# Output products end with the lower, then the upper columns; the third weight tile's low part goes behind the residual; three mixer units begin with a product in two halves

## The chip, the cores and the metric

The kernel runs on one core of a Trainium2 chip. The core has a matrix engine (TensorE, PE in the profile, with its weight loads as PEld), a vector engine (VectorE, DVE), a scalar engine (ScalarE, ACT), a general engine (GpSimd, POOL) and a queue engine for transfers (SyncE, SP). The metric is the device time of one execution, in microseconds (us); lower is better.

## What is computed

A decoder trunk of two layers on 256 positions of 1024 columns, in float32. Each layer is a half-step feed-forward block, a mixing block with two branches (a Mamba-2 style scan and a gated delta rule) on the same normalised input, and a second half-step feed-forward block.

```python
for l in range(DEPTH):                                   # DEPTH = 2
    h = h + 0.5 * swiglu(rms_norm(h, ffn1_norm[l]), ffn1_w_in[l], ffn1_w_out[l])
    u = rms_norm(h, mix_norm[l])
    (z_s, xbc, dt_s, qkv, z_d, b_d, a_d, gate_s, gate_d) = split(u @ w_in[l])
    y_s = mamba2_branch(z_s, xbc, dt_s, ...)
    y_d = deltanet_branch(qkv, z_d, b_d, a_d, ...)
    merged = sigmoid(gate_s) * (y_s @ ssm_w_branch[l]) + sigmoid(gate_d) * (y_d @ dn_w_branch[l])
    h = h + merged @ w_out[l]
    h = h + 0.5 * swiglu(rms_norm(h, ffn2_norm[l]), ffn2_w_in[l], ffn2_w_out[l])
return rms_norm(h, final_norm)
```

## The kernel before

**Weights.** All weights are streamed from memory once, as tiles of 128 x 1024 float32 (512 KB each). A tile is loaded into one of five raw buffers (`wraw`), and split into a high part `whi` (ScalarE, line 67) and a low part `wlo`, the raw tile less the high part (VectorE, line 70); there are five buffers of each. `prep` issues both; `take` hands a tile to the products and prepares the tiles ahead. Activations are split in the same way (`uW`, `gh`/`gl`, `mh`/`ml`). Every product of two matrices is three products on TensorE: high by high, high by low, low by high (`mm3` with 512 columns at a time, lines 318 to 320; `mm3w` with 256 columns, lines 323, 328 and 329).

**Two shapes of stage.** `tok_chunk` takes tiles in groups and multiplies both halves of the 256 positions (t = 0, then t = 1) by them, twelve products of 512 columns a tile. `chan_chunk` computes 256 channels for all positions from two tiles: 2 x 8 x 3 = 48 products of 256 columns, into one accumulator. The mixer's k, q, v, d, b and x units are each one `chan_chunk` (tiles `kk`, `qq`, `vv`, `zd`, `bc`, `xs` in the profile), its z and gate units `tok_chunk` (tile `t`). In the feed-forward blocks the `chan_chunk` products write `fc`.

**A product in two halves.** `mm3w(cut=True)` issues the second product of the three (high by low) as two products of 128 columns each (lines 325 and 326) instead of one of 256. `chan_chunk` does so once, at its fifth product (`a == 0 and kt == 1`), if it is asked to. Only the feed-forward blocks ask: for the third `fc` unit, and for the first one behind each group of block products.

**Output products and the joint.** A block ends with output products `o`: `out_chunks` takes the last five tiles (NSPL = 5) as one group, t = 0 first and then t = 1, into four accumulators `po[t][n]` (n = 0 the lower, n = 1 the upper 512 columns). For t = 0 all five tiles run for n = 0 and then for n = 1. For t = 1 each tile runs for n = 0 and then n = 1, unless `split` is set (only the last block of all). `state["sums"]` keeps each sum's last product; the transposes of t = 0 are held behind the sixth sum of t = 1, so that twelve products follow them.

Behind the output products comes what this document calls a joint (`norm_in` with `add`, five in the program: after the first feed-forward block of each layer, after each mixer, and between the layers). For each t: the residual add `h` for both n (VectorE, line 73), two squares (`junk`, ScalarE), a small add `zz` (VectorE), a power (`zz`, GpSimd), two scalings `hn` (VectorE), eight transposes `hnT` on TensorE (line 284), and the split of the transposed input into `uW` (high part ScalarE, low part VectorE). All of this has high priority in the scheduler that fixes the order of each engine's instructions when the program is built. The first tiles of the next stage are split around it: with n the index of the next stage's first tile, tiles n and n + 1 stand behind `hn` of t = 0, the third tile n + 2 behind `uW` of t = 0, the fifth tile n + 4 behind the squares and `hn` of t = 1; the fourth has no such edge. `tc.issue_after(ins)` adds an edge to the program's order: what is issued inside stands behind `ins` on the engine of `ins`.

**The mixer.** `ORDER` gives its units. Those around the change are, in the order of the program: `k1 k0 q1 k2 k3 K1 K0 q3 q0`, later `z30 v1 z31 Q2 v2 V0 I v3 V1 I V3 I Q1 V2 d0 R R R b3 R b2`, and later `S1 x20 T1 o x21`. A capital or single letter is a step without weights (transposes, small products, the inversion `I`, the recurrence `R`, the scan `S`/`T`). In the inversion 16 x 16 blocks go through memory, and come back as `T` and `TT`; the products `yb` read them.

Of the kernel before, what the change touches and what calls it, by code (L numbers as in the profile page):

```python
# [11 lines left out]
ALU = mybir.AluOpType  # L12
# [18 lines left out]
NSPL = 5  # L31
# [21 lines left out]
def trunk_kernel(ctx, tc, x, wst, wsm, norms, lpar, rpar, cst, out):  # L53
# [12 lines left out]
    def act(o, i, func=AF.Copy, **kw):  # L66
        return A.activation(out=o, in_=i, func=func, **kw)  # L67

    def tt(o, a, b, op):
        return V.tensor_tensor(out=o, in0=a, in1=b, op=op)  # L70

    def stt(o, a, s, b, op0, op1):
        return V.scalar_tensor_tensor(out=o, in0=a, scalar=s, in1=b, op0=op0, op1=op1)
# [6 lines left out]
    def f(ap):  # L80
        return ap.bitcast(F32)
# [67 lines left out]
    for _, _, need in plan:  # L149
        m, room = need, NRAW  # L150
# [4 lines left out]
            m += 1  # L155
        limit.append(m)
    n_forms = len(plan)
    state = {"loaded": 0, "prepped": 0, "taken": 0, "last": None, "hold": False, "behind": {}, "first": 0}
    raws, halves = {}, {}

    def tile_of(i):
# [2 lines left out]
    def add_to(r, i):  # L164
        G.dma_start(out=r[:], in_=tile_of(i), accum_op=ALU.add)  # L165
# [14 lines left out]
    def prep(i):  # L180
        kind, js, _ = plan[i]
        hi = wpool.tile([P, 1024], F32R, tag="whi", name="whi", bufs=NSPL)
        lo = wpool.tile([P, 1024], F32R, tag="wlo", name="wlo", bufs=NSPL)
        r = raws[js[0]]
        with ExitStack() as behind:
            for ins in state["behind"].pop(i, ()):
                behind.enter_context(tc.issue_after(ins))
            act(hi[:], r[:])
            if kind in ("q0", "q1"):
                to, by = (raws[k][:] for k in js[1:])  # L190
                tt(to, to, by, ALU.add)
            tt(lo[:], r[:], f(hi[:]), ALU.subtract)
        if kind == "q3":
            add_to(r, js[1])
        for k in {"q0": (js[0], js[-1]), "q1": (), "q3": ()}.get(kind, (js[0],)):
            raws.pop(k)
        halves[i] = (hi, lo)

    def ahead(key, n, fn):
        while state[key] < n:  # L200
            fn(state[key])
            state[key] += 1
# [88 lines left out]
    def norm_in(nw, add=None):  # L291

        place_input()
        for t in range(2):
            with tc.high_priority(offset=PRI), ExitStack() as behind:
                if add:
                    add(t)
                    if t == 0:
                        behind.enter_context(tc.issue_after(state["sums"][5].ins))
                ins, done = rms_chain(t, nw)  # L300
            if t == 0:
                state["hold"] = False
                n = state["taken"]
                if not add:
                    ahead("prepped", n + 1, prep)
                    with tc.issue_after(done[0].ins), tc.issue_after(done[1].ins):
                        ahead("prepped", n + START, prep)
                with tc.issue_after(ins.ins):
                    ahead("prepped", n + 2, prep)
                if add:  # L310
                    state["behind"][n + 2] = [d.ins for d in done]
            elif add:

                state["behind"][n + 4] = (state["square"].ins, ins.ins)
                state["input"] = done

    def mm3(ps, lh, ll, rh, rl, start, stop):
# [30 lines left out]
    def chan_chunk(ps, cut=False):  # L348

        ws = [take(), take()]  # L350
        for a in range(2):
            for q in range(2):
                wh, wl = ws[q]
                for k in range(4):
                    kt = 4 * q + k
                    c0 = k * 256 + a * P
                    mm3w(
                        ps[:, a * 256 : (a + 1) * 256],
                        wh[:, c0 : c0 + P],
                        wl[:, c0 : c0 + P],  # L360
                        uTh[:, kt, :],
                        uTl[:, kt, :],
                        kt == 0,
                        kt == KT - 1,
                        cut and a == 0 and kt == 1,
                    )

    def out_chunks(ps, stat, ks, last, group=1, split=False, first=None):

        for g0 in range(0, len(ks), group):  # L370
            kk = ks[g0 : g0 + group]
            ws = [(k, take()) for k in kk]
            for t in range(2):
                order = [(k, n) for n in range(2) for k in range(len(kk))]
                if t == 1 and not split:
                    order = [(k, n) for k in range(len(kk)) for n in range(2)]
                state["sums"] = []
                for k, n in order:
                    k, (wh, wl) = ws[k]
                    sh, sl = stat(k, t)  # L380
                    ins = mm3(
                        ps[t][n][:], sh, sl,
                        wh[:, n * 512 : (n + 1) * 512], wl[:, n * 512 : (n + 1) * 512],
                        k == 0 if first is None else first and t == n == 1, k == last,
                    )
                    state["sums"].append(ins)

    def residual(po, nw):
        def add(t):
            for n in range(2):  # L390
                hv = h[:, t, n * 512 : (n + 1) * 512]
                stt(hv, po[t][n][:], 0.5, hv, ALU.mult, ALU.add)

        if nw is None:
            return add
        norm_in(nw, add)
# [155 lines left out]
    def mixer(l, nxt):  # L552
# [201 lines left out]

        def k_unit(hp):
            ps = accb("kk")
            chan_chunk(ps)
            for a in range(2):
                conv(ps[:, a * S : (a + 1) * S], 2 * hp + a, kP[:, hp, :, a, :], False)

            def rest():
                ktb, nb = turned(kP, hp)
                ts(kq[:, hp], nb[:], EPS, ALU.add)
                c1 = small([P, 4], "c1")
                V.reciprocal(out=c1[:], in_=kq[:, hp])
                tt(c1[:], c1[:], Bp[:, hp], ALU.mult)
                stt(c3n[:, hp], c1[:], -1.0, eG[:, hp], ALU.mult, ALU.mult)
                kkb = trb("kkb")
                own(kkb, kP, kP, hp)
                kk = s2.tile([P, 4, 64], F32, tag="s2", name="kk")  # L770
                for c in range(4):
                    act(kk[:, c], kkb[:, c * 64 : (c + 1) * 64], scale=c1[:, c : c + 1])
                for a in range(2):
                    rows_ = slice(64 * a, 64 * a + 64)
                    qev["ins"] = tt(Q[rows_, 4 * hp : 4 * hp + 4, rows_], dN[rows_, 4 * hp : 4 * hp + 4], kk[rows_], ALU.mult)
                for c in range(3):
                    act(kd[:, c, hp, :], ktb[:, c * P : (c + 1) * P], scale=dT[:, 4 * hp + c, 63:64])
                rsqrt(c2[:, hp], kq[:, hp], [P, 4])
                G.tensor_tensor(out=c2[:, hp], in0=c2[:, hp], in1=Bp[:, hp], op=ALU.mult)
                yield  # L780

            return rest()
# [19 lines left out]

        def v_unit(hp):
            ps = accb("vv")
            chan_chunk(ps)
            vP = s2.tile([P, 4, 2, 64], F32, tag="s2", name="vP")
            for a in range(2):
                conv(ps[:, a * S : (a + 1) * S], 16 + 2 * hp + a, vP[:, :, a, :], False)

            def rest():  # L810
                vtb = trb("vtb")
                for c in range(4):
                    PE.transpose(vtb[:, c * P : (c + 1) * P], vP[:, c].rearrange("p a i -> p (a i)"), ident)
                for c in range(4):
                    act(vb[:, c, hp, :], vtb[:, c * P : (c + 1) * P], scale=c2[:, hp, c : c + 1])
                yield

            return rest()
# [167 lines left out]
        late = {}  # L986
# [49 lines left out]
        def xs_unit(g, i):  # L1036
            if i == 0:
                xsT[g] = slots.tile([P, 4, S], F32, tag=("sG", "sI")[g % 2], name="xsT")
            ps = accb("xs")
            chan_chunk(ps)  # L1040
            for a in range(2):
                conv(
                    ps[:, a * S : (a + 1) * S], 32 + 4 * g + 2 * i + a,
                    xsT[g][:, 2 * i + a].rearrange("p (c i) -> p c i", c=4), True,
                )
# [166 lines left out]
        m = tg[1]  # L1212
        ps = branch("s", 8, ss_T)
# [20 lines left out]
        po = [[accb("o"), accb("o")] for _ in range(2)]  # L1234
# [7 lines left out]
    for l in range(DEPTH):  # L1242
        ffn(norm_vec(3 * l + 1))
        mixer(l, norm_vec(3 * l + 2))
        add = ffn(norm_vec(3 * l + 3) if l + 1 < DEPTH else None)
# [145 lines left out]
```

## Time and profile before

| | |
|---|---|
| median of 3 runs | 1561.14 us (1560.59 to 1561.25) |
| profiled execution | 1561.29 us, its span 1559.5 us |
| TensorE busy | 1533.0 us, 98% of the span |
| VectorE busy | 1209.6 us, 78% |
| ScalarE busy | 945.0 us, 61% |
| TensorE clock granted, mean | 0.997 |

The profile shows one execution. Times in it count from the span's start. Each engine works through its own queue in a fixed order, and waits where an input of the next instruction isn't ready. Products on TensorE are pipelined: the time between two starts is the pace, and the duration of one is longer than that. `x64` is a count of instructions, and `<-` behind an idle time names what ended it.

### The profile page before, as it was taken

To read this page: it belongs to the slowest core of one execution; us is meant where nothing else is said; L and a number is where in the kernel's file an instruction comes from. 1 tells how busy PE (TensorE), PEld (TensorE's weight loads), DVE (VectorE), ACT (ScalarE), POOL (GpSimd) and SP (SyncE) were. 2 spreads that over 40 slices of the span, in tenths; PEclk is the share of its full clock that TensorE was granted. 3 is DMA by queue.
4 is the path that set the end of the run, shared out by engine and by line. 5 is a ranking of instruction groups with operands and counts; after the bars stand their busy time and mean duration, and the time that the engine had idled before them with its cause. 6 is when DMAs were issued, how large, how long until landed. Compare 5 with 4: busy or idle time off the path is not lost.

```text
span 1559.5 us, 29036 instructions
## 1 busy us (share of the span) xinstructions
PE 1533.0 (98%) x11452; PEld 1387.0 (89%) x11452; DVE 1209.6 (78%) x1840; ACT 945.0 (61%) x1534; POOL 95.9 (6%) x108
## 2 busy tenths in 40 slices
PE   8999999999999999999999999999999999999998
PEld 7999879999888888999789998899998888889996
DVE  5778868967899766778677787699579996667786
ACT  5555667766665645556555566686756665455564
POOL 0000110000000000000100011000000000000010
PEclk9999999999999999999999999999999999999999
DMA  8877765553565585577966687655435547856784
GB/s 287 257 251 237 246 213 181 171 163 116 180 207 173 179 255 193 185 251 228 323 209 205 219 257 238 200 188 176 132 123 199 193 161 221 247 173 197 231 251 155
DMA packets 103438, 322.50 MB, mean 207 GB/s; under 512 B 23349, under 2 KB 24325, under 8 KB 102278
## 3 DMA queue, kind: packets, MB, share of 16 engines
q1 hardware_dynamic: 96390, 299.68, 57.0%
q0 software_dynamic: 6912, 20.97, 7.8%
q8 instruction: 90, 1.47, 0.4%
q14 instruction: 46, 0.38, 0.1%
HBM read 314.50 MB, written 1.92 MB: 203 GB/s over the span
## 4 chain that ended last, share of the span: by engine, by line
PE 83%; DVE 7%; DMA 3%; issue 3%; ACT 3%; POOL 1%; SPq 0%; POOLq 0%; ACTq 0%; DVEq 0%
PE fc L329 9%; PE fc L323 9%; PE fc L328 9%; DVE wlo L70 3%; PE t L319 3%; PE t L318 3%; PE t L320 3%; PE b L320 3%; PE b L319 3%; PE b L318 2%; PE o L320 2%; PE o L319 2%; PE o L318 2%; DMA wraw<-in_wst_dram 2%; PE p L319 2%
## 5 line engine op out<-in xcount | busy, mean ns | idle before, releaser
L70 DVE TENSOR_TENSOR wlo<-wraw,whi 128x1024 fp32r<-128x1024 f32 x504 | 611.1, 1221 | 174.5 <-ACT whi L67 166.9
L67 ACT ACTIVATE whi<-wraw 128x1024 fp32r<-128x1024 f32 x504 | 527.1, 1058 | 273.9 <-PE fc L328 87.7
L329 PE MATMUL fc<-uW,wlo 128*128 128x256 f32 x1280 | 354.8, 277 | 0.0
L323 PE MATMUL fc<-uW,whi 128*128 128x256 f32 x1280 | 354.1, 277 | 0.0
L328 PE MATMUL fc<-uW,whi 128*128 128x256 f32 x1260 | 348.2, 276 | 0.0
L323 PEld LDWEIGHTS fc<-uW,whi 128*128 128x128 f32 x1280 | 240.3, 188 | 0.8
L329 PEld LDWEIGHTS fc<-uW,wlo 128*128 128x128 f32 x1280 | 240.5, 188 | 0.0
L328 PEld LDWEIGHTS fc<-uW,whi 128*128 128x128 f32 x1260 | 236.5, 188 | 0.8
L318 PE MATMUL t<-whi,uW 128*128 128x512 f32 x256 | 102.0, 400 | 0.0
L319 PE MATMUL t<-wlo,uW 128*128 128x512 f32 x256 | 100.7, 393 | 0.6 <-DVE wlo L70 0.4
L320 PE MATMUL t<-whi,uW 128*128 128x512 f32 x256 | 100.8, 394 | 0.0
L318 PE MATMUL b<-whi,bh 128*128 128x512 f32 x192 | 76.3, 399 | 0.3 <-ACT bh L67 0.3
L319 PE MATMUL b<-wlo,bh 128*128 128x512 f32 x192 | 74.9, 390 | 0.0
L320 PE MATMUL b<-whi,bl 128*128 128x512 f32 x192 | 74.3, 394 | 0.6 <-DVE bl L70 0.6
L323 PE MATMUL xs<-uW,whi 128*128 128x256 f32 x256 | 72.6, 284 | 0.0
L329 PE MATMUL xs<-uW,wlo 128*128 128x256 f32 x256 | 71.1, 278 | 0.0
L328 PE MATMUL xs<-uW,whi 128*128 128x256 f32 x256 | 70.9, 277 | 0.0
L70 DVE TENSOR_TENSOR wlo<-wsum,whi 128x1024 fp32r<-128x1024 f32 x48 | 58.6, 1221 | 14.7 <-ACT whi L67 13.8
L67 ACT ACTIVATE whi<-wsum 128x1024 fp32r<-128x1024 f32 x48 | 50.8, 1058 | 28.4 <-PE fc L328 23.8
L318 PE MATMUL o<-whi,gh 128*128 128x512 f32 x160 | 63.8, 399 | 1.9 <-ACT whi L67 1.9
L319 PE MATMUL o<-wlo,gh 128*128 128x512 f32 x160 | 63.9, 399 | 1.6 <-DVE wlo L70 1.6
L165 POOL DMA_DIRECT2D wsum<-in_wst_dram x32 | 28.1, 878 | 584.3 <-DVE wlo L70 455.1
(320 smaller groups left out, 3429.8 us busy)
## 6 DMA issues: line engine op xcount, KB each, us to landing
wraw<-in_wst_dram SPq DMA_DIRECT2D x520, 512.0 KB, 5.0
wsum<-in_wst_dram POOLq DMA_DIRECT2D x32, 512.0 KB, 7.3
wsum<-in_wst_dram SPq DMA_DIRECT2D x16, 512.0 KB, 7.1
dc<-rdram SPq DMA_DIRECT2D x8, 1024.0 KB, 9.1
nw<-in_norms_dram SPq DMA_DIRECT2D x6, 512.0 KB, 6.3
h<-u POOLq DMA_DIRECT2D x12, 256.0 KB, 6.8
gb<-rdram SPq DMA_DIRECT2D x8, 256.0 KB, 5.7
h<-in_x_dram SPq DMA_DIRECT2D x4, 256.0 KB, 3.0
```

Of the source, the lines that this page charges most:

```text
L67: return A.activation(out=o, in_=i, func=func, **kw)
L70: return V.tensor_tensor(out=o, in0=a, in1=b, op=op)
L165: G.dma_start(out=r[:], in_=tile_of(i), accum_op=ALU.add)
L318: PE.matmul(ps, lh, rh, start=start, stop=False)
L319: PE.matmul(ps, lh, rl, start=False, stop=False)
L320: return PE.matmul(ps, ll, rh, start=False, stop=stop)
L323: PE.matmul(ps, wh, mh, start=start, stop=False)
L328: PE.matmul(ps, wh, ml, start=False, stop=False)
L329: PE.matmul(ps, wl, mh, start=False, stop=stop)
```

## The change

Three things are changed.

1. For t = 1 of a group of five output tiles, the first three tiles still run n = 0, n = 1 each; the last two run both for n = 0 (the lower columns), then both for n = 1 (the upper columns). The sum of the lower columns is complete six products before the end instead of three.
2. `residual`'s `add` returns its last instruction, and `norm_in` keeps that of t = 1 under the index of the third tile of the next stage. When this tile is prepared, the instructions behind that point, the low part on VectorE above all, stand behind the residual add in VectorE's order.
3. `chan_chunk` is asked for the product in two halves in units k1, v2 and x20 of the mixer, in both layers: six more products in the program.

```diff
@@ prep
+            if i in state["late"]:
+                behind.enter_context(tc.issue_after(state["late"].pop(i).ins))
             tt(lo[:], r[:], f(hi[:]), ALU.subtract)
@@ norm_in
                 if add:
-                    add(t)
+                    added = add(t)
...
                 state["behind"][n + 4] = (state["square"].ins, ins.ins)
+                state["late"][n + 2] = added
@@ out_chunks
                 order = [(k, n) for n in range(2) for k in range(len(kk))]
                 if t == 1 and not split:
-                    order = [(k, n) for k in range(len(kk)) for n in range(2)]
+                    m = len(kk) - 2 if len(kk) == NSPL else len(kk)
+                    order = [(k, n) for k in range(m) for n in range(2)]
+                    order += [(k, n) for n in range(2) for k in range(m, len(kk))]
@@ residual: add
-                stt(hv, po[t][n][:], 0.5, hv, ALU.mult, ALU.add)
+                ins = stt(hv, po[t][n][:], 0.5, hv, ALU.mult, ALU.add)
+            return ins
@@ k_unit
-            chan_chunk(ps)
+            chan_chunk(ps, hp == 1)
@@ v_unit
-            chan_chunk(ps)
+            chan_chunk(ps, hp == 2)
@@ xs_unit
-            chan_chunk(ps)
+            chan_chunk(ps, (g, i) == (2, 0))
```

More of the change, by code (lines that the diff above doesn't have):

```diff
@@ L157, in trunk_kernel @@
     n_forms = len(plan)
-    state = {"loaded": 0, "prepped": 0, "taken": 0, "last": None, "hold": False, "behind": {}, "first": 0}
+    state = {"loaded": 0, "prepped": 0, "taken": 0, "last": None, "hold": False, "behind": {}, "late": {}, "first": 0}
     raws, halves = {}, {}
```

## The prediction

> **What bounds the kernel now.** I read the page first (engine shares, then the chain that ended last), then TensorE's own waits, then the timeline at the five joints (places where output products end and the next stage begins), then TensorE's products unit by unit in the two mixers.
>
> ```profile
> span 1559.5 us, 29036 instructions
> PE 1533.0 (98%) x11452; PEld 1387.0 (89%) x11452; DVE 1209.6 (78%) x1840; ACT 945.0 (61%) x1534; POOL 95.9 (6%) x108
> PE 83%; DVE 7%; DMA 3%; issue 3%; ACT 3%; POOL 1%; SPq 0%; POOLq 0%; ACTq 0%; DVEq 0%
> ```
>
> TensorE is busy for 98% of the span and carries 83% of the chain. So time comes off in only two ways: TensorE waits less, or its products follow each other faster. The change tries both. The list of TensorE's waits, from 10 us on (so without the start), has one row for the joints:
>
> ```profile
> PE hnT L284 <- DVE hn L73: 4.3, 5, 0.9
> ```
>
> Five waits, one for each joint with a residual before a norm, 4.3 us in all. The timeline of the first joint (start, duration, engine, line, output<-inputs) shows how it arises:
>
> ```profile
> 181.05 13.02 SPq L177 DMA_DIRECT2D wraw<-in_wst_dram  x4
> ...
> 190.75 2.01 ACT L67 ACTIVATE whi<-wraw 128x1024 fp32r<-128x1024 f32 x2
> 191.31 1.28 DVE L70 TENSOR_TENSOR uW<-hnT,uW 128x512 fp32r<-128x512 f32 x2
> 192.51 1.21 DVE L70 TENSOR_TENSOR wlo<-wraw,whi 128x1024 fp32r<-128x1024 f32 x1
> 192.53 0.39 PE L320 MATMUL o<-whi,gl 128*128 128x512 f32 x1
> 192.76 0.39 PE L318 MATMUL t<-whi,uW 128*128 128x512 f32 x1
> 193.64 1.28 DVE L73 SCALAR_TENSOR_TENSOR h<-o,h 128x512 f32<-128x512 f32 x2
> 194.84 1.21 DVE L70 TENSOR_TENSOR wlo<-wraw,whi 128x1024 fp32r<-128x1024 f32 x1
> 195.73 0.39 PE L319 MATMUL t<-wlo,uW 128*128 128x512 f32 x1
> 195.97 0.20 DVE L78 TENSOR_SCALAR zz<-ss 128x1 f32<-128x1 f32 x1
> 196.42 0.40 PE L319 MATMUL t<-wlo,uW 128*128 128x512 f32 x1
> 196.90 1.42 DVE L73 SCALAR_TENSOR_TENSOR hn<-h,zz,nw 128x512 f32<-128x512 f32 x2 [0.73 <-POOL zz L212]
> 197.71 0.66 PE L284 MATMUL hnT<-cs,hn 128*128 128x128 f32 x4 [0.89 <-DVE hn L73]
> ```
>
> The last output product starts at 192.53 and ends at 192.92. VectorE is then in the third tile's low part (192.51 to 193.72), so both residual adds (h) run at 193.64 to 194.92. The fourth tile's low part follows, then zz, then hn. TensorE started its last product before the transposes at 196.42. At the pace of these rows, 0.23 us, the transposes could have started at 196.65; they start at 197.71, 1.06 us late.
>
> **Part one: the joints.** With the new edge VectorE goes from uW straight to the residual. The left half's sum is complete by then (it was, three products before the end; now six before), so the first add can run at 192.5; the second needs the last product, 192.92, and its place behind the first, so it starts at about 193.1 and ends at about 193.8: 1.1 us earlier than 194.92. The reordering of the last two tiles is thus worth nothing by itself here: VectorE is the later of the two for the left half. The third low part now fills the place that the fourth had between the adds and zz, with the same 1.21 us, so zz also moves by 1.1 us, to about 194.85. Then VectorE has a gap of 0.73 us until hn, in which the fourth low part is now ready; being 1.21 us long it would push hn from 195.8 to about 196.15. That is 0.75 us earlier than 196.90; without the filling it is 1.06 us, the whole wait.
>
> What lies against it is TensorE's order. It is fixed at build time by a scheduler that lets ready work of high priority go first, and the transposes have such priority. Where its plan also has hn earlier, it puts the transposes before fewer products than the 17 of now (192.76 to 196.42), and each product fewer gives 0.23 us back. The plan did see room for a low part ahead of the adds, so it held them ready later than VectorE was free; the plan's own gain lies between 0 and the 1.1 us of the chip. So a joint pays between 0 (the order follows in full) and 1.06 us (it stays and nothing fills the gap). I take 0.45 us, the 0.75 us less one or two products: 5 x 0.45 = 2.2 us.
>
> Covers: the third low part would end at about 195.0 instead of 193.72, and its first user starts at 195.73 (thirteen products of 0.23 us after 192.76): hidden by 0.7 us. Its end frees a raw buffer, so SP's fourth load in the row at 181.05 goes out 1.2 us later, with the two small parameter loads queued behind it on SP. Each tile lasts TensorE twelve products, 2.7 us, and this load's tile is used after four others, so this is covered. The fourth tile's high part (second ACT of the row at 190.75) waits for the buffer of the fourth output tile, whose last use moves from six to three products before the end, 0.68 us: it would end at about 193.3, before the squares need ScalarE (after the first add, 193.2). Nothing if that holds, 0.1 us on the squares if not. A new wait on VectorE (the third low part behind the adds) stands ahead of zz only.
>
> **Part two: the halves.** The same products run at two paces. In the view of one tile's instructions (count: min/median/max ns, first to last start), the k units of layer 0 and layer 1, each with the q1 unit between them, 240 products:
>
> ```profile
> L323 PE MATMUL kk<-uW,whi x64: 281/281/364, 233.2 to 261.2; 128*128 128x256 f32 x64
> L329 PE MATMUL kk<-uW,wlo x64: 281/281/283, 233.5 to 261.4; 128*128 128x256 f32 x64
> L323 PE MATMUL kk<-uW,whi x64: 276/276/367, 1006.1 to 1033.1; 128*128 128x256 f32 x64
> L329 PE MATMUL kk<-uW,wlo x64: 276/276/279, 1006.5 to 1033.3; 128*128 128x256 f32 x64
> ```
>
> 233.2 to 261.4 is 28.2 us, 118 ns each over 239 steps; 1006.1 to 1033.3 is 27.2 us, 113.8 ns: 4.2 ns apart, and the durations tell them apart too (281, 276). The kernel already has such halves in its FFNs. The timeline of one:
>
> ```profile
> 103.67 0.28 PE L323 MATMUL fc<-uW,whi 128*128 128x256 f32 x1
> 103.79 0.22 PE L325 MATMUL fc<-uW,whi 128*128 128x128 f32 x1
> 103.85 0.28 PE L326 MATMUL fc<-uW,whi 128*128 128x128 f32 x1
> ...
> 104.49 0.28 PE L323 MATMUL fc<-uW,whi 128*128 128x256 f32 x1
> 104.60 0.28 PE L328 MATMUL fc<-uW,whi 128*128 128x256 f32 x1
> 104.72 0.28 PE L329 MATMUL fc<-uW,wlo 128*128 128x256 f32 x1
> 104.83 0.28 PE L323 MATMUL fc<-uW,whi 128*128 128x256 f32 x1
> ```
>
> The step ahead of it is 0.12 us; those from 104.49 to 104.83 are 0.113 us. From the first half at 103.79 to 104.49 are the five products of the kernel without halves (the halved one and four more): 0.70 us against 5 x 118 = 0.59 us slow or 0.57 us fast. So a cut costs 0.11 us in a slow stretch and 0.13 us in a fast one, and it pays 4.2 ns on every slow product behind it until other work comes between.
>
> Unit k1, layer 0: the cut is the fifth product; of 240 some 231 lie behind the five steps: 231 x 4.2 = 0.97, less 0.11: gain 0.86 us. Layer 1 is fast already: loss 0.13 us. Unit v2 opens a stretch v2, v3, d0, b3 and the first part of b2:
>
> ```profile
> L323 PE MATMUL vv<-uW,whi x32: 281/281/281, 307.4 to 318.4; 128*128 128x256 f32 x32
> L323 PE MATMUL bc<-uW,whi x23: 280/281/281, 324.4 to 332.1; 128*128 128x256 f32 x23
> L323 PE MATMUL vv<-uW,whi x32: 281/281/281, 1079.3 to 1090.2; 128*128 128x256 f32 x32
> L323 PE MATMUL bc<-uW,whi x23: 280/281/281, 1096.2 to 1104.0; 128*128 128x256 f32 x23
> L846 SPq DMA_DIRECT2D TT<-dq x8: 440/447/1569, 321.5 to 329.5; - x8
> DMA to landing us min/median/max: 1.7/1.8/1.9
> ```
>
> Slow in both layers, 211 products from 307.4 to 332.1; 201 x 4.2 = 0.84, less 0.11: 0.73 us, twice 1.46 us. What comes next on TensorE reads TT, whose last transfer is issued at 329.5 and lands 1.8 us later, at 331.3; the stretch's last product starts at 332.1 and the next step comes 0.2 us later, 1.0 us after the landing, so 0.73 us fits. If that cover were gone, the gain would be a wait.
>
> Unit x20 is cut where TensorE waits soon after for something else:
>
> ```profile
> 451.62 0.44 PE L1061 MATMUL xsb<-cs,xsT 128*128 128x128 f32 x2 [0.67 <-ACT xsT L67]
> ```
>
> The 0.13 us lie in this wait, and so does the faster pace of the few products before it: 0. If the wait goes elsewhere, 0.13 us lost a layer, or up to 0.1 us gained.
>
> Sum of the halves: 0.86 - 0.13 + 1.46 = 2.2 us. Bounds: if the k stretch of layer 0 came out fast by itself, 1.46 - 0.26 = 1.2 us, less 0.26 us for x20: 0.9 us. If layer 1's came out slow without the cut, 2.2 us stays, since the cut only returns it to its old pace.
>
> The Trainium skill, "TensorE: Matmul & The Clock Gate", section "Back-to-back issue gap", gives a warm product one gap, N / 2.4 + 2.5 ns: 109 ns for 256 columns, and two halves cost 2.5 ns more than a whole. By that page there is no slower pace to leave; the rows above differ from it, with 118 and 113.8 ns for one and the same form.
>
> **Sum.** 2.2 + 2.2 = 4.4 us. The profiled execution took 1561.29 us (span 1559.5), 0.15 us above the median of the runs, 1561.14; taken off the median this is 1556.7 us.
>
> **The rivals.**
> (1) The transposes move up with hn and the joints pay nothing; the halves pay: 1561.1 - 2.2 = 1558.9 us. For it: priority order. Against: the plan and the chip would have to gain alike. 0.17.
> (2) One pace: halves do not move the pace in the mixer, where other work set it, and six cuts cost 0.11 to 0.13 us each, 0.7 us; the joints pay: 1559.6 us. Against: layer 1's fast k stretch and the cut at 103.79. 0.06. The Trainium skill's rule above, carried to this kernel, says the same.
> (3) Slower: the third low part falls behind hn. Once it may not go ahead of the adds, VectorE's order can put zz and both hn before it. It would then start at about 197.3 and end at 198.5, while its user stands at 195.73: TensorE waits 2.8 us there instead of 1.06 us at the transposes, 1.7 us more a joint, 8.7 us in all, less 2.2: 1567.6 us. It decides from the point where the low part ends after 196.8. Where a longer wait also drops the clock it costs more; the row of stretches (length, PE, PEld, DVE, ACT, POOL busy, granted clock, DMA share, GB/s) shows this before another joint:
>
> ```profile
> 766.00:774.00 8.00, 4.89 (x16) 2.62 (x15) 4.10 (x4) 2.56 (x3) 0.86 (x1) 0.86 1.05 301
> 774.00:779.00 5.00, 5.00 (x13) 3.85 (x13) 0.69 (x1) 0.72 (x2) 0.86 (x1) 0.54 1.03 382
> ```
>
> 3.1 us idle in 8 us were followed by 5 us at 0.54 of the clock: 2.3 us lost. Against this rival: VectorE stands idle for the squares just then, and a low part fits there. 0.12.
> (4) The edge changes nothing, because another wait ends last at the joints, and moved work eats the halves: 1561 us. 0.05.
>
> **How the numbers follow.** 0.2% (3.1 us) is about what a measurement of this kernel can tell from no change, so faster means under 1558.0 us, slower over 1564.3 us. The forecast (both parts pay, joints 0.25 to 1.06 us each) has 0.60: with joints at 1.06 it gives 1561.1 - 5.3 - 2.2 = 1553.6; with joints at 0.25 and halves at 0.9 it gives 1558.9. Of it 0.57 is below 1558.0. Same: 0.03 + 0.17 + 0.06 + 0.05 = 0.31. Slower 0.12. The range takes in the forecast and rivals 1, 2 and 4, and leaves out rival 3: 1553.4 to 1561.5 us.
>
> **What would show it.** Right: at each joint h directly behind uW on VectorE, the third low part behind h, and the wait row for hnT well under 4.3 us; the k stretch of layer 0 and both v2 stretches with medians of 276 ns, and 27.2 us instead of 28.2 us for the first; the yb products behind b2 without a new wait. Wrong: fewer than 17 products between joint and transposes with the wait unchanged (rival 1); 281 ns behind a cut (rival 2); a wait of TensorE for wlo in the first stage after a joint (rival 3). A loss of several us elsewhere, as at 766 to 779 us, where loads set the pace, would be outside all of these.

## The result and the profile after

The changed kernel takes 1556.39 us in the median of 14 runs (1554.38 to 1559.58), the kernel before 1560.64 us beside it (14 runs, 1559.26 to 1563.55). The ratio is 0.9973, with a 95% interval of 0.9965 to 0.9982: 4.2 us faster, between 2.8 and 5.5 us. The profiled execution took 1555.2 us. The head of its page:

```profile
span 1553.4 us, 29029 instructions
PE 1529.5 (98%) x11458; PEld 1384.0 (89%) x11458; DVE 1210.0 (78%) x1840; ACT 945.9 (61%) x1534; POOL 100.7 (6%) x108
```

TensorE has six more products (the halves) and is still busy for 98% of the span. One number is odd: GpSimd does the same 108 instructions and is busy for 4.8 us longer (95.9 before). The joints explain 4.4 us of it: one power of each takes 0.84 to 0.91 us longer. The first joint in the timeline after (start, duration, engine, line, output<-inputs, idle before):

```profile
188.98 1.28 DVE L70 TENSOR_TENSOR uW<-hnT,uW 128x512 fp32r<-128x512 f32 x2
190.00 1.06 ACT L67 ACTIVATE whi<-wraw 128x1024 fp32r<-128x1024 f32 x1 [0.51 <-ACT whi L67]
190.18 1.28 DVE L73 SCALAR_TENSOR_TENSOR h<-o,h 128x512 f32<-128x512 f32 x2
190.21 0.39 PE L323 MATMUL o<-whi,gl 128*128 128x512 f32 x1
190.43 0.39 PE L321 MATMUL t<-whi,uW 128*128 128x512 f32 x1
190.97 0.61 ACT L67 ACTIVATE junk<-h 128x512 f32<-128x512 f32 x1
191.38 1.22 DVE L70 TENSOR_TENSOR wlo<-wraw,whi 128x1024 fp32r<-128x1024 f32 x1
192.51 0.21 DVE L78 TENSOR_SCALAR zz<-ss 128x1 f32<-128x1 f32 x1
192.63 1.21 DVE L70 TENSOR_TENSOR wlo<-wraw,whi 128x1024 fp32r<-128x1024 f32 x1
192.86 1.39 POOL L214 TENSOR_TENSOR zz<-zz,mhalf 128x1 f32<-128x1 f32 x1 [7.52 <-DVE zz L78]
194.29 1.42 DVE L73 SCALAR_TENSOR_TENSOR hn<-h,zz,nw 128x512 f32<-128x512 f32 x2 [0.44 <-POOL zz L214]
194.33 0.39 PE L323 MATMUL t<-whi,uW 128*128 128x512 f32 x1
195.10 0.44 PE L286 MATMUL hnT<-cs,hn 128*128 128x128 f32 x2 [0.38 <-DVE hn L73]
```

Count from the start of the last output product (192.53 before, 190.21 after). The residual `h` now stands directly behind `uW`, the third low part behind `h`, and `zz` comes 2.30 us after that product instead of 3.44: 1.14 us earlier. Then the gain shrinks: `hn` comes at 4.08 instead of 4.37, only 0.29 us earlier. Between the two, the power on GpSimd lasts 1.39 us, beside the fourth low part (192.63 to 193.84); before it lay in VectorE's gap and took 0.56 us. TensorE puts one product more ahead of the transposes: 194.33 is the eighteenth (before: seventeen). So the wait is 195.10 less 194.56 (194.33 and one pace of 0.23): 0.54 us instead of 1.06. TensorE's waits from 25 us on show the same at all five joints (us in total, times, longest):

```profile
PE o L322 <- DVE wlo L70: 2.5, 5, 0.8
PE o L321 <- ACT whi L67: 2.4, 3, 1.7
PE hnT L286 <- DVE hn L73: 1.9, 5, 0.4
PE xsb L1067 <- ACT xsT L67: 1.9, 2, 0.9
```

4.3 us of `hnT` have become 1.9. The first two rows are waits of output products for weight tiles, nearly all in the stretch before the third joint, which the change does not touch; they come back below. The last row, in front of which unit x20 stands, was 1.3 us before:

```profile
PE xsb L1061 <- ACT xsT L67: 1.3, 2, 0.7
```

The k products of both layers and v2 of both layers, by tile (count: min/median/max ns, first to last start):

```profile
L326 PE MATMUL kk<-uW,whi x64: 275/276/367, 229.7 to 256.8; 128*128 128x256 f32 x64
L332 PE MATMUL kk<-uW,wlo x64: 276/276/333, 230.0 to 257.0; 128*128 128x256 f32 x64
L326 PE MATMUL kk<-uW,whi x64: 276/276/367, 1001.2 to 1028.3; 128*128 128x256 f32 x64
L331 PE MATMUL vv<-uW,whi x39: 276/276/286, 294.7 to 313.8; 128*128 128x256 f32 x39
L326 PE MATMUL vv<-uW,whi x41: 276/276/281, 1065.8 to 1085.2; 128*128 128x256 f32 x41
```

All have medians of 276 ns, with a halved product in each stretch. The k stretch lasts 27.31 us in both layers (28.23 and 27.19 before); from v2's first product to the first `yb` 24.04 us in both (24.94 before). That is 0.92 us gained, 0.12 lost, and twice 0.90 gained. These are the lengths that Part two of the prediction foresaw; the experiments show which of them the halves brought about, and under what condition.

### The profile page after: what moved, and what is told of

Same layout as the page of the kernel before. It is cut to its first block, busy times and chain, and to the rows that moved or that the text cites. A ratio compares the mean times of both kernels' runs of the same rounds, so it can differ in the third digit from the quotient of the medians.

```text
span 1553.4 us, 29029 instructions
## 1 busy us (share of the span) xinstructions
PE 1529.5 (98%) x11458; PEld 1384.0 (89%) x11458; DVE 1210.0 (78%) x1840; ACT 945.9 (61%) x1534; POOL 100.7 (6%) x108
## 3 DMA queue, kind: packets, MB, share of 16 engines
q8 instruction: 90, 1.47, 0.4%
## 4 chain that ended last, share of the span: by engine, by line
PE 82%; DVE 6%; DMA 4%; issue 3%; ACT 3%; POOL 1%; SPq 0%; POOLq 0%; ACTq 0%; DVEq 0%
PE fc L332 9%; PE fc L326 9%; PE fc L331 9%; PE t L321 3%; PE t L322 3%; PE t L323 3%; DMA wraw<-in_wst_dram 3%; PE b L323 3%; PE b L321 3%; PE b L322 3%; PE o L323 2%; PE o L322 2%; PE o L321 2%; DVE wlo L70 2%; PE p L322 2%
```

## Experiments: which part pays

Three kernels first: the halves alone, the joints alone (edge and order), and edge with halves but the old order of the output products.

**The halves alone.**

```diff
-                state["late"][n + 2] = added
...
-   m = len(kk) - 2 if len(kk) == NSPL else len(kk)
-   order = [(k, n) for k in range(m) for n in range(2)]
-   order += [(k, n) for n in range(2) for k in range(m, len(kk))]
+   order = [(k, n) for k in range(len(kk)) for n in range(2)]
```

> The kernel before with the three units' halves alone. Theory (both parts pay by themselves): the k stretch of layer 0 comes to 27.2 us from 28.2, both stretches from v2 to b2 come 0.8 us shorter, layer 1's k stretch loses 0.1 us; TensorE's five waits for hnT stay at 4.3 us with 17 products ahead of the transposes; 2.2 us faster than before, ratio 0.9986. Rival (the joints carry it all and the halves' gain is given back as waits behind b2): stretches shorter but the time within 0.5 us of before, ratio 0.9997 to 1.0003.

Measured: 1560.04 us (11 runs), ratio to before 0.9985 (0.9975 to 0.9996): 2.3 us, the size that the theory had. Whether the halves are its cause is the matter of the section on the pace.

**The joints alone.**

```diff
-            chan_chunk(ps, hp == 1)
+            chan_chunk(ps)
...
-            chan_chunk(ps, hp == 2)
+            chan_chunk(ps)
...
-            chan_chunk(ps, (g, i) == (2, 0))
+            chan_chunk(ps)
```

> The change without the three units' halves: reordered output products and the edge of the third low part. Theory: the five waits for hnT fall from 4.3 to 1.9 us in all, 18 products ahead of the transposes instead of 17, 0.5 us a joint, 2.5 us faster than before, ratio 0.9984; GpSimd's power at the joints takes 1.4 us instead of 0.56, as in the changed kernel, since a low part runs on VectorE beside it. Rival (the halves carry it all; the wait moves to the output products): ratio 0.9997 to 1.0003 with waits of output products grown by 2 us.

Measured: 1556.95 us (11 runs), ratio 0.9974 (0.9962 to 0.9985): as much as the whole change, within the intervals.

**Without the new order.**

```diff
-   m = len(kk) - 2 if len(kk) == NSPL else len(kk)
-   order = [(k, n) for k in range(m) for n in range(2)]
-   order += [(k, n) for n in range(2) for k in range(m, len(kk))]
+   order = [(k, n) for k in range(len(kk)) for n in range(2)]
```

> The changed kernel with the old order of the last two output tiles, so the edge and the halves alone. Theory (VectorE is the later of the two for the lower columns, so the order is worth nothing by itself): h starts directly behind uW as in the changed kernel, waits for hnT at 1.9 us, the fourth high part runs without its wait of 0.5 us; within 0.5 us of the changed kernel, ratio to before 0.997. Rival (the order lets h into the gap): h starts 0.4 us or more later, waits for hnT 3 us or more, ratio 0.9985.

Measured: 1555.49 us (8 runs), ratio 0.9970 (0.9956 to 0.9983). Its joints are those of the changed kernel, eighteen products and all. The new order is worth nothing that these runs can see.

**Without the edge** (new order and halves stay).

```diff
-                state["late"][n + 2] = added
```

> The changed kernel without the edge of the third low part, so the order and the halves alone. Theory (the edge is what takes the low part out of the way): the third low part runs ahead of at least one of the two residual adds, waits for hnT stay near 4.3 us (3.5 or more), ratio to before 0.9986. Rival (the new order alone lets both adds go first): waits at 1.9 us and the ratio of the changed kernel, 0.997.

Measured: 1560.54 us (11 runs), ratio 0.9990 (0.9980 to 1.0000). TensorE's wait at the joints, a row of the kernel with the halves alone (the kernel without the edge has the same one) and a row of the kernel without the new order (1.9 us in the kernel with the joints alone):

```profile
PE hnT L286 <- DVE hn L73: 4.4, 5, 0.9
```
```profile
PE hnT L286 <- DVE hn L73: 2.0, 5, 0.4
```

4.4 us wherever the edge is missing, 1.9 to 2.0 wherever it is there. The edge carries the joints: 2.4 us of the 4.2. Without it, the new order lets the first residual add go ahead of the third low part, but `zz` still comes 3.44 us after the last output product.

## Experiments: why the joint pays 0.5 and not 1.1 us

Theory: the fourth low part on VectorE holds up the power on GpSimd, and so `hn`. The fourth low part was therefore put behind the last `hn` of t = 1.

```diff
                 state["late"][n + 2] = added
+                state["late"][n + 3] = ins
```

> The changed kernel with one more edge: the fourth tile's low part behind the last hn of t = 1, so that VectorE is idle while GpSimd computes the power. Theory (the low part on VectorE holds up GpSimd's power): the power at t = 1 takes 0.56 us again instead of 1.4, hn starts 0.9 us earlier, waits for hnT near 0; the fourth low part ends about 0.9 us before its user needs it or up to 0.3 us late; 1.0 to 2.5 us faster than the changed kernel, ratio to before 0.9957 to 0.9967. Rival (the power is slow for another reason, its place in the queue or the load beside it): it stays at 1.4 us, and the late low part costs 0.3 us a joint, ratio 0.998.

The ten powers of the five joints (min/median/max ns) before, after, and in this kernel, one row each:

```profile
L212 POOL TENSOR_TENSOR zz<-zz,mhalf x10: 548/559/566, 187.1 to 1377.9; 128x1 f32<-128x1 f32 x10
```
```profile
L214 POOL TENSOR_TENSOR zz<-zz,mhalf x10: 559/980/1474, 184.8 to 1370.7; 128x1 f32<-128x1 f32 x10
```
```profile
L214 POOL TENSOR_TENSOR zz<-zz,mhalf x10: 550/561/568, 185.6 to 1372.2; 128x1 f32<-128x1 f32 x10
```

After, the median lies between two groups: five powers at about 0.56 us (t = 0) and five at 1.39 to 1.47 us (t = 1, with the low part beside them). With the low part gone all ten are at 0.56 again: shown. By the Trainium skill, "SBUF — State Buffer", section "SBUF: two separate sides", an instruction of VectorE with two inputs in SBUF and one of GpSimd that reads SBUF share a port pair; who comes first holds it for the whole instruction. The traces agree that the later one is held: `wlo` has two such inputs and began 0.23 us before the power, which ended 0.41 us behind it (194.25 against 193.84). That is less than the 0.56 us of a whole power, so the trace does not show at which point of the power the hold lies.

But the kernel took 1558.64 us (10 runs), ratio 0.9976 (0.9965 to 0.9987), no faster than the change. Its first joint in the timeline says why:

```profile
191.01 0.39 PE L324 MATMUL o<-whi,gl 128*128 128x512 f32 x1
191.24 0.39 PE L322 MATMUL t<-whi,uW 128*128 128x512 f32 x1
193.63 0.55 POOL L214 TENSOR_TENSOR zz<-zz,mhalf 128x1 f32<-128x1 f32 x1 [7.51 <-DVE zz L78]
194.21 0.40 PE L323 MATMUL t<-wlo,uW 128*128 128x512 f32 x1
194.22 1.41 DVE L73 SCALAR_TENSOR_TENSOR hn<-h,zz,nw 128x512 f32<-128x512 f32 x2 [0.73 <-POOL zz L214]
195.02 1.32 PE L286 MATMUL hnT<-cs,hn 128*128 128x128 f32 x8 [0.41 <-DVE hn L73]
```

`hn` now comes 3.21 us after the last output product, 1.16 us earlier than before the change. But between 191.24 and 194.21 stand fourteen products instead of eighteen: the transposes moved up with it, and TensorE waits for 0.58 us again (195.02 less 194.44). What `hn` gained, TensorE's order gave back: rival 1's mechanism, here in a kernel that frees the power. The total wait at the joints is 2.1 us, where this experiment's theory had next to nothing.

## Experiments: the pace of the products

In the kernel with the joints alone, which has no halves in the mixer, the k products of layer 0 and the v2 products of layer 1 read:

```profile
L326 PE MATMUL kk<-uW,whi x64: 276/276/367, 229.1 to 256.1; 128*128 128x256 f32 x64
L326 PE MATMUL vv<-uW,whi x32: 281/281/281, 1074.9 to 1085.9; 128*128 128x256 f32 x32
```

So k of layer 0 was fast without a cut. Is the pace then a matter of the program, or of the execution? The kernel before was run twice more, and the kernel with the joints alone once more.

> The kernel before once more, for its profile. Theory (the pace of a stretch without halves is settled anew in each execution): one of the four stretches (k and v2 to yb in both layers) shows the other pace than in the first profile, where they took 28.2, 27.2, 24.9 and 24.9 us. Rival (the pace is settled by the program): all four again within 0.1 us.

> The kernel with the joints' part alone once more, for its profile. Theory (pace settled anew in each execution): one of the four stretches shows the other pace than in its first profile, where they took 27.2, 27.2, 24.1 and 25.2 us. Rival (settled by the program): all four again within 0.1 us.

> The kernel before a third time, for its profile. Theory (pace settled anew in each execution): the k stretch of layer 0 is at 27.2 us in most executions and 28.2 in some, the stretches from v2 to yb at 24.1 or 24.9 us, not the same set as in either earlier profile. Rival (the first profile was the rule): 28.2, 27.2, 24.9, 24.9.

They took 1562.79, 1556.93 and 1561.29 us (one run each). The kernel before, run again, k and v2 of layer 0:

```profile
L323 PE MATMUL kk<-uW,whi x64: 276/276/367, 234.7 to 261.7; 128*128 128x256 f32 x64
L323 PE MATMUL vv<-uW,whi x40: 276/276/282, 299.8 to 318.8; 128*128 128x256 f32 x40
```

The same program that ran k of layer 0 and v2 at 281 ns in the first profile ran both at 276 ns in this one. (The kernel with the joints alone kept the pace of each of its four stretches in its second profile: there the theory's guess missed.) The lengths in us, L0 then L1, of each profile of the three programs without halves in k and v2, and of those with:

| profile | k stretch | v2 to yb |
|---|---|---|
| before | 28.23, 27.19 | 24.94, 24.94 |
| before, again | 27.19, 27.17 | 24.06, 25.60 |
| before, third | 27.19, 27.17 | 24.35, 24.43 |
| joints alone | 27.19, 27.17 | 24.06, 25.16 |
| joints alone, again | 27.17, 27.17 | 24.09, 24.94 |
| nine kernels with the halves | 27.30 to 27.31 in all 18 | 24.04 in 13 of 18, 24.14 to 24.93 in five |

So one program can run the same stretch at either pace. Call a stretch fast where its products have a median of 276 ns and slow where it is 281. Without a cut, k was slow in one of ten stretches and v2 in four of ten. With a cut, k was fast in all 18, but v2 was slow in two of 18: in layer 1 of the kernel with the `wsum` loads held and of the kernel without the halves in x20 (both further down), where the halved product stands in its place and all that follows runs at 281 ns. The last product ahead of v2 and the products of v2 in the latter kernel (count: min/median/max ns):

```profile
L323 PE MATMUL t<-whi,uW x1: 393/393/393, 1076.7 to 1076.7; 128*128 128x512 f32 x1
```
```profile
L332 PE MATMUL vv<-uW,wlo x32: 281/281/333, 1077.1 to 1088.2; 128*128 128x256 f32 x32
L328 PE MATMUL vv<-uW,whi x1: 223/223/223, 1077.4 to 1077.4; 128*128 128x128 f32 x1
```

In the changed kernel, with the same cut, the product ahead is shorter and the stretch is fast:

```profile
L323 PE MATMUL t<-whi,uW x1: 389/389/389, 1074.3 to 1074.3; 128*128 128x512 f32 x1
```
```profile
L332 PE MATMUL vv<-uW,wlo x32: 276/276/332, 1074.7 to 1085.4; 128*128 128x256 f32 x32
```

And in layer 1 of the kernel before, run again, there is no cut, a product of 393 ns stands ahead, and the stretch is fast by itself from its sixth product on:

```profile
L320 PE MATMUL t<-whi,uW x1: 393/393/393, 1080.0 to 1080.0; 128*128 128x512 f32 x1
```
```profile
L329 PE MATMUL vv<-uW,wlo x32: 276/276/281, 1080.4 to 1091.0; 128*128 128x256 f32 x32
```

The duration of the product ahead sorts all 28 v2 stretches:

| last product ahead of v2 | without a cut | with a cut |
|---|---|---|
| 389 ns | slow in 4 of 4 | fast in 15 of 15 |
| 392 ns | fast in 3 of 3 | fast in 1 of 1 |
| 393 ns | fast in 3 of 3 | slow in 2 of 2 |

The rest of the program agrees. Over all 14 profiles, take every row of 36 products or more of 256 columns that follows a product of 512 columns without a pause, the feed-forward blocks included. Behind 387 to 391 ns all 45 without a cut were slow and all 232 with one fast; behind 392 to 398 ns all 40 without a cut were fast, and of ten with one six were slow. So the cut does move the pace, and in both directions: whether it pays goes with how the stretch is entered, which the duration of the product ahead tells. Behind 389 ns it takes v2 from 24.94 to 24.04 us; behind 393 ns it costs about as much (24.93 us, against 24.09 in the second profile of the joints alone). This sorts what the executions happened to do; no kernel was made to enter at 389 or at 393 ns. What sets the entry is open, and so is whether the chip has a part in it, since the groups of runs were on different chips; layers 0 and 1 of one execution can differ. For k nothing is shown: its one slow stretch began with a product of 364 ns, all others with 362 or 367, and no cut one began with 364.

In the mean k is worth nothing (27.28 without, 27.31 with), and v2 0.5 us a layer (24.66 without, 24.17 with; 15 of the 18 with a cut entered at 389 ns, 4 of the 10 without). The 25.60 and the 24.35 show that the cover the prediction named, the landing of `TT` 1.0 us ahead of its reader, is sometimes gone. TensorE's waits in the second and in the third profile of the kernel before:

```profile
PE yb L851 <- DMA TT<-dq: 1.5, 1, 1.5
```
```profile
PE yb L851 <- DMA TT<-dq: 0.6, 2, 0.3
```

**Unit x20.** The row for `xsb` grew from 1.3 to 1.9 us. The halves of x20 were taken out of the changed kernel:

```diff
-            chan_chunk(ps, (g, i) == (2, 0))
+            chan_chunk(ps)
```

> The changed kernel without the halves in x20, for its profile. Theory (the extra instruction moves the transposes two products up into their wait): 23 instructions ahead of the waiting transposes again instead of 21, the wait 0.8 to 0.95 us instead of 1.2, and the unit with its transposes 0.35 us shorter in each layer, 7.2 to 7.5 us. Rival (x20's halves cost nothing): 7.7 to 7.9 us as in the changed kernel.

Measured: 1558.44 us in one run, too few for the total. TensorE's wait is 1.2 us again (0.7 longest):

```profile
PE xsb L1067 <- ACT xsT L67: 1.2, 2, 0.7
```

The unit with its transposes took 7.49 and 7.29 us, against 7.5 to 7.9 us in the kernels with these halves and 7.2 to 7.5 in those without. With the halves, TensorE's order has 21 instructions ahead of the waiting transposes instead of 23. The added half moved the transposes up into their own wait, and products that had filled it now come behind: the 15 products of `xs` among the 21 are 14 whole ones, 17 stood there before, and three at 0.118 us each are 0.35 us.

## Experiments: the loads before the third joint

Both kernels lose several us in the output products between the layers. A window of after there (length; PE, PEld, DVE, ACT, POOL busy; granted clock; DMA share; GB/s):

```profile
768.10:774.80 6.70, 5.68 (x13) 4.12 (x14) 1.92 (x2) 1.22 (x3) 0.86 (x1) 0.50 1.04 353
```

Between 760 and 770 us TensorE waits for `whi` and `wlo` in seven pieces of 0.2 to 1.7 us, 4.8 us in all. And from 768.0 to 774.9 us the granted clock is at 0.50; half of these 6.8 us, 3.4 us, is lost as well. All eleven profiles in which this stretch stalls have such a piece at 0.50 in it, of 6.8 us (10.2 in one); the three in which it doesn't (below) have none there.

The DMA issues of after in 740 to 780 us (KB each, median us to landing) suggest a cause: beside twelve weight tiles, seven loads into `wsum` for the first block of layer 1 (three plain ones on SyncE, four on GpSimd that add to them), which are needed only behind the joint.

```profile
wraw<-in_wst_dram SPq DMA_DIRECT2D x12, 512.0 KB, 10.9
wsum<-in_wst_dram POOLq DMA_DIRECT2D x4, 512.0 KB, 8.8
wsum<-in_wst_dram SPq DMA_DIRECT2D x3, 512.0 KB, 12.5
```

First try: every `wsum` load of SyncE kept behind the load ahead of it in the stream, so that the scheduler cannot issue it early.

```diff
+            if state["last"] is not None:
+                with tc.issue_after(state["last"].ins):
+                    state["last"] = nc.sync.dma_start(r[:], tile_of(i))
+                raws[j] = r
+                return
```

> The changed kernel with the loads of the summed tiles (wsum, issued on SP) held in SP's order behind the weight tile ahead of them in the stream, so that the next block's sums are not loaded during the output products between the layers. Theory (these early loads crowd out the weight tiles there): the output products ahead of the third joint take 31 us instead of 41 to 43, their waits for whi and wlo go from 4.9 us to under 1 us; 6 to 10 us faster than the changed kernel, ratio to before 0.991 to 0.993. Rival (the loads are needed by then, and wait later): the same time lost at the block products of the next feed-forward block, ratio 0.997.

Measured: 1568.91 us (6 runs), ratio 1.0045 (1.0028 to 1.0061): slower. The stretch itself is cured (33.6 us from the first output product to the joint, 42.9 in after), so the early loads do cause the loss there. But in the feed-forward blocks the loads now come too late:

```profile
PE fc L337 <- DVE wlo L70: 8.3, 4, 2.9
```

Second try: only the four `wsum` loads of layer 1's first block, the first behind the load of layer 0's last output tile, each other one five weight tiles later.

```diff
...
+    opened, gates = {}, {}
...
+    third = [j for j in range(n_raw) if stream[j][0] == "y"][8:12]
+    tail = [j for j in range(third[0]) if stream[j][0] == "w" and stream[j][1] < j0 // 2][-1]
+    ahead_w = [j for j in range(tail, n_raw) if stream[j][0] == "w"]
+    gates.update({y: min(ahead_w[g], y - 1) for y, g in zip(third, (0, 5, 10, 15))})
...
+            with ExitStack() as behind:
+                if j in gates:
+                    behind.enter_context(tc.issue_after(opened[gates[j]].ins))
+                nc.sync.dma_start(r[:], tile_of(i))
...
-        state["last"] = nc.sync.dma_start(r[:], tile_of(i))
+            state["last"] = nc.sync.dma_start(r[:], tile_of(i))
+            if j in gates.values():
+                opened[j] = state["last"]
```

> The changed kernel with only the four early loads between the layers moved: the loads of the summed tiles of the second layer's first block go out behind the last output tile of the first layer and then behind every fifth weight tile. Theory (they crowd out the weight tiles of the output products, and are not needed before 840 us): the output products ahead of the third joint take 33.6 us instead of 41 to 43, and no new waits come in the block behind them; 7 to 9 us faster than the changed kernel, ratio to before 0.991 to 0.993. Rival (the same bytes only come later): the stall appears among the fc products of the next block, 2 to 3 us each, ratio 0.996 to 1.000.

Measured: 1549.5 us (5 runs, 1546.09 to 1550.79), ratio to before 0.9918 (0.9903 to 0.9933). TensorE has no new wait among the `fc` products. The weight tiles of 740 to 780 us land sooner, and there are more of them:

```profile
wraw<-in_wst_dram SPq DMA_DIRECT2D x16, 512.0 KB, 6.1
wsum<-in_wst_dram SPq DMA_DIRECT2D x2, 512.0 KB, 8.6
wsum<-in_wst_dram POOLq DMA_DIRECT2D x2, 512.0 KB, 8.9
```

The output products by tile, a row of after and one of this kernel: 40.8 us from first to last start, and 31.7 us for the same forty.

```profile
L321 PE MATMUL o<-whi,gh x40: 388/389/796, 742.4 to 783.2; 128*128 128x512 f32 x40
```
```profile
L332 PE MATMUL o<-whi,gh x40: 388/389/473, 743.8 to 775.5; 128*128 128x512 f32 x40
```

The maximum falls from 796 to 473 ns as well: the granted clock is 1.00 there all along. Nine us less in this profile, of which the waits (4.8) and the clock (3.4) are some 8; 6.9 us between the medians of the two kernels, 8.6 by their ratios to before.

Last, this kernel without the halves of x20 (the edit shown above).

> The kernel with the four transfers held back, without the halves in unit x20 alone. If those halves cost 0.35 us a layer, because the added product moves the transposes of the B rows up into their wait: the two x20 units get shorter by 0.35 us each (from 7.5 to 7.9 us down to 7.2 to 7.5), TensorE's wait for them goes from 0.9 to 0.7 us, and the whole stands 0.7 us lower, about 1548.8 us, ratio 0.991 to 0.992. If the added product only fills a wait (the prediction's reading): no difference in the units beyond 0.1 us. The output products ahead of the third joint last 33.7 us again and wait for no weight tile, if that was the four transfers and not chance.

Measured: 1548.82 us (4 runs, 1547.05 to 1551.04), ratio to before 0.9906 (0.9890 to 0.9923): the lowest median of all. The x20 units take 7.49 and 7.38 us against 7.85 and 7.73 with the halves, 0.36 and 0.35 us less. The medians differ by 0.7 us, but their intervals overlap; that the total gains is seen in the units only.

## Why the prediction came out right, and where it did not

The forecast was 1556.7 us, the median is 1556.39. That the two lie so close is in part luck: the joints came out about as forecast because two errors made up for each other, and the halves are worth 0.3 us by the traces, where 2.2 us were forecast.

- **TensorE bounds, only waits and pace count**: held. What is shown of the gain is a wait that shrank and products that follow each other faster.
- **Residual and zz 1.1 us earlier, the order worth nothing**: held, 1.14 us, and the kernel without the new order is as fast.
- **hn 0.75 us earlier, because the fourth low part fills the gap**: the part does fill the gap, but the size was off. It measured 0.29 us at the first joint (0.23 to 0.29 at the five). The step reckoned the low part's 1.21 us against VectorE's time alone; it also held up the power on GpSimd, from 0.56 to 1.39 us.
- **Less one or two products, since the transposes move up**: wrong sign. They stand one product later, which adds 0.23 us. 0.29 + 0.23 = 0.52 us at the first joint (2.5 us at the five), where 0.75 less 0.30 gave 0.45: two terms were mis-sized and made up for each other. Rival 1 was not what happened here, but the kernel with the fourth tile late shows its mechanism at work.
- **Covers**: TensorE does not wait for the third or fourth tile's low part in the first stage. The fourth tile's high part starts behind 0.51 us of idle time and ends at 191.06, and the first square starts some 0.1 us late: the prediction's "0.1 us on the squares if not".
- **Halves, 0.86 - 0.13 + 1.46 us**: right in the profile at hand (0.92, -0.12, 1.80 between the two profiles) and wrong as a statement about the program. Two steps failed. One execution's pace was taken for the kernel's; the lower bound considered a fast k of layer 0, but not fast v2 stretches. And "it pays 4.2 ns on every slow product behind it" holds where the stretch begins behind a product of 389 ns; behind 393 ns the cut itself made v2 slow, in two stretches of 18. In the mean, k gives 0 and v2 0.5 us a layer.
- **Unit x20, 0**: it costs 0.35 us a layer. "The 0.13 us lie in this wait" overlooked that the transposes would come earlier in TensorE's order.
- **Rivals**: rival 2 (one pace) is wrong as a mechanism, since a cut does move the pace in the mixer, though its sign, 281 ns behind a cut, came in two stretches. It is nearer than the forecast in what the halves are worth: twice 0.5 less twice 0.35, 0.3 us by these profiles. Rival 3 did not come about: the low part ran in the squares' time, where the prediction saw the gap. Rival 4 is out.
- **The loss outside all the cases, at 766 to 779 us**: it is in both kernels. From the first output product to the third joint it took 40.6 to 41.4 us in three profiles of the kernel before, and 41.0 to 42.9 in eight kernels with the change or parts of it; up to 1 us may be given back there. The prediction read 2.3 us lost to the clock from its two windows; at 0.50 from 771.7 to 778.6 us it is 3.4 us. As its own subject this loss was the largest of all, 7 to 9 us.
- **The page's one gap of 109 ns** (the Trainium skill, "TensorE: Matmul & The Clock Gate", section "Back-to-back issue gap"): no stretch ran at it, with halves or without; none was below 113 ns. The section gives this formula for an isolated product, and says that in a stream of weight loads and products both set the spacing; the prediction left that out. The price of a cut estimated from it, 2.5 ns, is far from the 0.11 to 0.13 us of the traces, so what rival 2 reckoned and what follows from the page are not quite the same.

What stays open: the joints give 2.4 to 2.5 us by the traces, the halves 0.3 us in the mean of single profiles, and the runs say 4.2 us (2.8 to 5.5) for the whole. The joints alone give 4.1 us by their runs (2.3 to 5.9), the halves alone 2.3 us (0.6 to 3.9), but on top of the joints next to nothing (0.9973 against 0.9974). The sum of the two lies above the whole, though not outside what the intervals allow. The loads of the start and of the stretch before the third joint differ from profile to profile by 1 us and more, so that the last microsecond or two cannot be placed. Why the scheduler put the transposes at eighteen and at fourteen products was not tried either.

## What to carry to other kernels

Before a gap of an engine is filled, look at what the other engines do in it: here a small power on GpSimd lost most of what the vector engine gained. Profile the same program more than once before a pace is taken for a property of the program, and look at what stands ahead of a stretch: the same cut made one stretch faster and another slower. In a kernel whose matrix engine is at 98%, read the stretches where it waits for loads first, since transfers that nobody needs yet can cost more than all the joints.

## What the hardware showed that was not expected

- A power on 128 x 1 values takes 0.56 us by itself and 1.39 to 1.47 us when a VectorE instruction with two inputs in SBUF has begun just ahead of it, in five of the ten powers at the joints of the changed kernel, and in none when that instruction was moved away.
- The same products of 256 columns run at 113.4 or at 118 ns each, in one and the same program. Directly behind a product of 512 columns the duration of that product tells which: behind 387 to 391 ns 45 of 45 stretches without a cut were slow and 232 of 232 with one fast; behind 392 to 398 ns 40 of 40 without a cut were fast, and six of ten with one slow. What sets the duration ahead was not found.
- Seven early loads of 512 KB among twelve weight tiles put the tiles' landing at 10.9 us (median of the stretch), four among sixteen at 6.1 us. In the first case TensorE waited in seven pieces, none over 1.7 us, and the clock was at 0.50 for 6.8 us; in the second it did not wait and the clock stayed at 1.00.
